# An attention layer whose turned keys lie with their tokens side by side, and whose half-zero query tiles are kept

## The chip, the cores and the metric

The kernel runs on one core of a Trainium2 chip. Its engines are TensorE (PE, with its weight loads as PEld), VectorE (DVE), ScalarE (ACT), GpSimd (POOL), and SyncE (SP), which here only issues transfers; 16 DMA engines move data between DRAM and the core's memory. The metric is the time on the device in microseconds (us), median of several executions.

## The reference

One decoder layer over 1024 tokens of width 1024, in 32-bit floats: a token mixer of attention heads beside a short gated convolution, then a squared-ReLU MLP.

```python
z = rms_norm(x, g_mix_norm) @ w_in          # q, six k/v pieces, gates, conv channels
q = rms_norm(q.reshape(B, T, 8, 64), g_q)   # 8 heads of 64, 2 groups of keys
k_cmp = rms_norm(compress(kc, ...), g_k[0]) # one key per 16 tokens, from blocks of 32
k_slc = rms_norm(ks_, g_k[1])               # selected branch: the 16 best blocks of 64 tokens
k_win = rms_norm(kw_, g_k[2])               # window branch: the last 512 tokens
o = gate0 * softmax(q k_cmp) v_cmp + gate1 * softmax(q k_slc) v_slc + gate2 * softmax(q k_win) v_win
mixed = concat(rms_norm(o, g_out[:512]), rms_norm(conv_out, g_out[512:]))
x = x + mixed @ w_o
x = x + square(relu(rms_norm(x, g_ffn_norm) @ w_up)) @ w_down
```

With 1024 tokens there are only 16 blocks of 64, so the selected branch takes all of them. The softmax scores carry a penalty for distance, and everything is causal.

## The kernel before, in words

**Arithmetic.** A product of 32-bit floats is made of three matmuls: each operand is split into a rounded high part and the rest, and high x high, high x low and low x high are added (`mm3`). Where a tile is called `...h` and `...l`, these are the two parts.

**Stages.** The tokens are taken in 8 blocks of 128. First the input projection (`z_tokens`, and the products `zZ`, `zX`, `zW` for the convolution's channels), with the work on keys and values beside it. Then attention: for each block and group, scores on PE, softmax on DVE, ACT and POOL, turns of the probabilities on PE (`tp`), and their product with the values (`ot`). Then the output projection and the MLP (`X` and `Z` products with `we`, `uu`), which takes about half of the time.

**Keys.** `k_norm` (line 843) normalises the keys of one block of 128 tokens for one branch (`krow`, 128 tokens x 128 numbers: 2 halves of 32 dimensions for 2 groups), and turns them on DVE in squares of 32 x 32 into `kturn`, of which there is one buffer. One store per block and branch puts `kturn` into the DRAM tile `k_d` (line 680), 512 bytes per partition. There are 16 such stores of 64 KB. `v_split` stores the values in the same manner into `v_d`. Before attention, lines 1186 to 1196 load everything back: the keys into four tiles `kn` (two branches x two halves of 512 tokens: `kn00` and `kn01` are the selected branch, `kn10` and `kn11` the window branch), four loads of 128 KB each, 32 partitions with 16 pieces of 256 bytes; the values into `vs` and `vw`, 1 MB each. `split_keys` (line 1204) rounds a `kn` tile into the high part `KH` on ACT and puts the rest into `KL` on DVE, once for each group, so eight times in all.

**Queries.** `queries` (line 1318) loads four pieces `qx` per block and group, copies them into `Qg` (the queries' high part in one half of the partitions, the low part in the other), and makes `Qz`, of which only the group's own half is filled: it clears the other half on POOL, then copies the own one from `Qg`. `Qz` is a ring of two buffers; each of the 16 tiles is cleared anew.

**Scores.** `scores` (line 1234) multiplies `KH` by `Qg` and `KL` by `Qz` into an accumulator `s_`, of which there are two. DVE reads it, adds the penalty and takes the maximum (`pt`, with `nm` the negative maximum), and ACT takes the exponential. PE can't start a third score before DVE has read the first.

**`wc`.** The output projection of the convolution's half (line 1360 on) doesn't need attention. Its 192 matmuls are spread among the first scores. They need `rconv`, made from a few short products `s_<-ones,sqs`. The results are added to tiles `xt` or `y`, which are loaded from x.

**What sets the order.** Every operation is recorded as a node (`Plan`, line 156 on), so almost everything shows as line 273 in the profile and must be told apart by its tiles. A planner (`best`, line 581) then builds an order for all engines by a list schedule, with a cost for each operation and a reckoning of when each transfer lands; `plan.slack` (line 490) adds to that landing, in the reckoning alone. The numbers in `SEEDS` (line 153) each shake the priorities of some operations at random, one after another (`shaken`, line 565). The result is emitted as it stands: every engine takes its instructions in that order. SP issues nearly all loads and stores in one queue in order; a load whose tile isn't free yet holds up all that stand behind it. The `kn`, `qx` and `V` tiles take the space of tiles that the products `zZ` use, so the first of these loads waits until the last `zZ` is done.

Of the kernel before, what the change touches and what calls it, by code (L numbers as in the profile page):

```python
# [10 lines left out]
F32 = mybir.dt.float32  # L11
F32R = mybir.dt.float32r
# [7 lines left out]
P = 128  # L20
T = 1024
# [4 lines left out]
G = 2  # L26
R = H // G
HD = 64
AW = H * HD
CW = D - AW  # L30
NCMP = T // 16
# [118 lines left out]
        self.seen, self.nodes, self.tile = [], [], None  # L150


SEEDS = (1, 23, 31, 38, 41, 62, 71, 73, 75, 77, 80, 88, 104, 105, 109, 117, 124, 125, 127, 128, 139, 177, 192, 197, 199, 200, 266, 277, 284, 301, 314, 374, 375, 379, 394, 395, 403, 428, 451, 473, 489, 497, 527, 539, 602, 635, 663, 668, 683, 688, 735, 738, 757, 795, 807, 960, 974, 981, 1033, 1087, 1174, 1207, 1227, 1240, 1266, 1330, 1456, 1463, 1494, 1514, 1524, 1530, 1663, 1704, 1707, 1772, 1800, 1878, 2113, 2223, 2390, 2423, 2489, 2544, 2549, 2570, 2574, 2706, 2765, 2808, 2860, 2976, 2978, 3198, 3470, 3483, 3569, 3710, 3726, 3799, 3961, 4024, 4169, 4173, 4281, 4302, 4454, 4464, 4536, 4631, 4816, 4942, 5475, 5732, 5800, 5998, 6019, 6274, 6308, 6361, 6542, 6590, 6629, 6638, 6652, 6763, 6768, 6849, 6898, 6926, 6933, 7427, 7431, 7843, 8840, 8935, 9098, 9312, 9425, 9449, 9490, 9543, 9796, 10243, 10373, 10450, 10719, 10753, 10755, 10988, 11031, 11263, 11298, 11337, 11378, 11468, 11734, 11858, 11860, 12512, 12525, 12556, 12899, 12910, 12948, 13367, 13696, 13855, 13915, 13972, 14164, 15272, 15349, 15386, 15617, 16147, 16281, 16952, 16985, 17425, 17652, 17676, 17915, 18093, 18097, 18255, 18325, 18342, 18702, 18971, 19150, 19474, 19616, 21193, 21235, 21388, 21680, 21948, 22334, 23213, 23339, 23611, 23843, 24118, 24207, 24710, 24756, 24876, 25684, 25805, 26155, 26173, 26856, 27014, 28405, 28909, 29650, 29975, 30412, 30442, 30461, 30772, 31961, 32809, 33604, 33968, 34207, 35108, 35382, 35516, 35716, 35789, 36229, 36353, 36557, 36875, 38880, 39359, 39872, 39943, 39989, 40863, 40948, 40951, 41904, 43210, 43597,)


class Plan:
# [437 lines left out]
    def issue(self):  # L594
        end, order = self.schedule(self.best(SEEDS)[1])
        if len(order) < len(self.nodes):
            raise Exception("not all scheduled")
        self.end = end
        with self.tc.manual_schedule(engines=ENGINES):
            for n in order:  # L600
                for f in n.do:
                    f()
        self.done = True
# [3 lines left out]
def trunk_layer(ctx, tc, x, x_t, vectors, w_in, g_qk, w_cmp1, b_cmp1, w_cmp2, b_cmp2,  # L607
                w_o, w_up, w_down, out):
    plan = Plan(tc)
    nc = plan.nc  # L610
# [18 lines left out]
    def copy_act(o, i, scale=1.0):  # L629
        nc.scalar.activation(o, i, AF.Copy, scale=scale)  # L630
# [37 lines left out]
    def rsqrt(o, ss, n, scale):  # L668
        t = st.tile([P, n], F32, name="rs_t", tag=f"rs{n}")
        nc.vector.tensor_scalar(t, ss, scale, EPS, op0=ALU.mult, op1=ALU.add)  # L670
        nc.gpsimd.tensor_tensor(o, t, mhalf[:, :n], op=ALU.pow)

    yacc = {}
    dram = pool(ctx, "dram", space=DRAM)
# [2 lines left out]
    x1_d = dram.tile([T, D], F32, name="x1_d")  # L677
    x2_d = dram.tile([T, D], F32, name="x2_d")
    t_d = dram.tile([T, D], F32, name="t_d")
    k_d = [dram.tile([T, G * HD], F32, name=f"k_d{br}") for br in range(2)]  # L680
    v_d = {br: dram.tile([T, G * 2 * HD], F32, name=f"v_d{br}") for br in "sw"}
    u_d = [dram.tile([7, P, 512], F32, name=f"u_d{q}") for q in range(NPAIR)]

# [158 lines left out]
    with b1:  # L842
        def k_norm(src, br, tb):
            dst = zt.tile([P, 2, G, 32], F32, name="krow")
            sq = zt.tile([P, HD], BF16, name="ksq", bufs=2)
            ss = st.tile([P, G], F32, name="kss")
            for g in range(G):
                c = slice(g * HD, (g + 1) * HD)
                nc.scalar.activation(sq, src[:, c], AF.Square, accum_out=ss[:, g:g + 1])
            ri = st.tile([P, G], F32, name="kri")  # L850
            rsqrt(ri, ss, G, 1.0 / HD)
            for g in range(G):
                nc.vector.scalar_tensor_tensor(dst[:, :, g], src[:, g * HD:(g + 1) * HD].rearrange("p (j d) -> p j d", j=2),
                                               ri[:, g:g + 1], gk_bc[:, br].rearrange("p (j d) -> p j d", j=2),
                                               op0=ALU.mult, op1=ALU.mult)
            turned = zt.tile([P, G * HD], F32, name="kturn", bufs=1)
            nc.vector.transpose(turned, dst.rearrange("p j g d -> p (j g d)"))
            nc.sync.dma_start(k_d[br - 1][tb * P:(tb + 1) * P], turned)

        def v_split(src, br, tb):  # L860
            v = zt.tile([P, G, 2, HD], F32R, name="vrow")
# [112 lines left out]
        for tb, ps in (a for tbs in (QUADS[1], (0,), (1,), (2,), (3,)) for a in z_tokens(pieces, tbs, 512, steps, 1)):  # L974
# [4 lines left out]
            for h in range(H):  # L979
                c = slice(h * HD, (h + 1) * HD)  # L980
# [40 lines left out]
    with ExitStack() as b2:  # L1021
# [10 lines left out]
        def half_tile(name):  # L1032
            return cz.tile([P, 512], F32, name=name, tag="ct", bufs=3)
# [100 lines left out]
        for c in (0, 2):  # L1134
            vs = [u_pair(c + i) for i in range(2)]
            v = [[a[:, th * 512:(th + 1) * 512] for th in range(2)] for a in vs]
            for name, ps in channels(C_CONV + 2 * CW + c * P, C_CONV + 2 * CW + (c + 1) * P):
# [14 lines left out]
                elif name == "S1":  # L1152
                    a = half_tile("ca")
# [28 lines left out]
        def y_tile(shape, name):  # L1182
            return yp.tile(shape, F32, name=name, tag="y", bufs=6)

        V = {br: vp.tile([P, NT, G, 2, HD], F32R, name=f"v{br}", tag=f"v{br}") for br in "sw"}
        kn = {}
        for qd in range(2):
            for br in range(2):
                kn[br, qd] = y_tile([P, 16, G, 32], f"kn{br}{qd}")
                for c in range(4):  # L1190
                    nc.sync.dma_start(kn[br, qd][c * 32:(c + 1) * 32].rearrange("p t g d -> p t (g d)"),
                                      k_d[br][qd * 512:(qd + 1) * 512, c % 2 * HD:c % 2 * HD + HD].rearrange(
                                          "(t p) n -> p t n", p=32))
        for br in "sw":
            nc.sync.dma_start(V[br].rearrange("p t g a d -> p t (g a d)").bitcast(F32),
                              v_d[br].rearrange("(t p) n -> p t n", p=P))
        kp_stack = ExitStack()
        kp = pool(kp_stack, "kp")
        KW = NCMP + 2 * T
# [2 lines left out]
        half = [slice(g * HD, (g + 1) * HD) for g in range(G)]  # L1202

        def split_keys(g, c0, n, ps):
            kh, kl = KH[g][:, c0:c0 + n], KL[:, c0:c0 + n]
            if n == 512:
                kh, kl = [a.rearrange("p (t d) -> p t d", d=32) for a in (kh, kl)]
            copy_act(kh, ps)
            tt(nc.vector, kl[half[g]], ps[half[g]], kh[half[g]].bitcast(F32), ALU.subtract)
        d_sw = kp.tile([P, 1152], F32, name="d_sw")  # L1210
# [8 lines left out]
                                base=0, channel_multiplier=-1)  # L1219

        def k_transposes(g, br, qd):
            split_keys(g, NCMP + br * T + qd * 512, 512, kn[br, qd][:, :, g])

        plan.plus = 20.0
        for g in range(G):
# [4 lines left out]
        psC = pool(cps_stack, "psC", space=PSUM, side="right")  # L1230
        psS_stack = ExitStack()
        psS = pool(psS_stack, "psS", bufs=2, space=PSUM)
        q_load = []
        def scores(tb, g, Qt, filler, po=640):
            Qg, Qz = Qt
            W = (tb + 1) * P
# [81 lines left out]
        def queries(tb):  # L1318
            Qs = []
            for g in range(G):  # L1320
                qx = kp.tile([P, 4, R, 32], F32, name="qx", bufs=1)
                for c in range(4):
                    q_load.append(nc.sync.dma_start(
                        qx[c * 32:(c + 1) * 32].rearrange("p b r t -> p b (r t)"),
                        q_d[tb * P:(tb + 1) * P, (4 * g + c) * P:(4 * g + c + 1) * P].rearrange("(b p) n -> p b n", b=4)))
                Qg = kp.tile([P, R, P], F32R, name="Qg", bufs=3)
                Qz = kp.tile([P, R, P], F32R, name="Qz", bufs=2)
                copy_act(Qg.rearrange("p r (b t) -> p b r t", b=4), qx)
                nc.gpsimd.memset(Qz[half[1 - g]].bitcast(F32), 0.0)
# [18 lines left out]
        for it, tb in [*enumerate(ORDER)][6:] + [*enumerate(ORDER)][:6]:  # L1348
            xt = xq.tile([P, D], F32, name="xt") if it >= 6 else y_tile([P, D], f"y{tb}")
            nc.sync.dma_start(xt, x2d[tb * P:(tb + 1) * P])  # L1350
            t = slice(tb * P, (tb + 1) * P)
            for nh in range(2):
                n = slice(nh * 512, (nh + 1) * 512)
                tag, bufs = (("ot", 2), ("ot", 2), ("ms", 1))[(it * 2 + nh) % 3]
# [28 lines left out]
    with ExitStack() as c_:  # L1383
# [280 lines left out]
        for tb in late[:-1]:  # L1664
            t = ez.tile([P, 512], F32, name="t", tag="t")
# [144 lines left out]
    for c in range(NPAIR // CHUNK):  # L1810
# [6 lines left out]
        for p in range(7):  # L1817
# [17 lines left out]
            ih, n = ACC[p]  # L1835
            for j in range(4):
# [58 lines left out]
```

## Time and profile before

| what | value |
| --- | --- |
| median of 3 runs | 1191.03 us (1188.57 to 1192.53) |
| profiled execution, its own time | 1190.73 us |
| its span, first instruction to last | 1189.0 us |
| granted clock of PE, mean | 0.997 |
| loads of `kn`: 16 of 128 KB, median from issue to landing | 5.3 us |
| stores of `k_d`: 16 of 64 KB, the same | 2.3 us |
| loads of `qx`: 64 of 64 KB, the same | 2.1 us |
| clears of `Qz` on POOL: 16, mean | 521 ns |

The page's groups give an engine, an operation and its tiles (numbers left out), the count, the busy time and the mean of one. Rows of windows give for each engine the busy time and, in brackets, the number of instructions; then the granted clock (PEclk, 1.00 is full), the share of the DMA engines (over 1 where packets overlap) and GB/s. A row of waits names the instruction that waited, what it waited for, and the total, the count and the longest in us. Rows of the timeline and of the chain begin with start and length in us.

### The profile page before, as it was taken

How to read it: one execution, taken by the hardware profiler on the slowest of the kernel's cores; microseconds unless marked ns; L12 is line 12 of the kernel's file. 1: busy time of each engine (PE TensorE's matmuls, PEld its weight loads, DVE VectorE, ACT ScalarE, POOL GpSimd, SP SyncE). 2: the span in 40 equal slices, each digit the busy share in tenths (PEclk: the TensorE clock that was granted, in tenths of full speed). 3: DMA queues.
4: the chain of work that ended last, by engine and by line, in shares of the span. 5: the costliest groups of instructions: out<-in, count | busy, mean ns of one | idle time of the engine just before them, and what ended most of it. 6: DMA issues, size and time to landing. Idle time of an engine off the chain costs nothing.

```text
span 1189.0 us, 18003 instructions
## 1 busy us (share of the span) xinstructions
PE 1176.9 (99%) x5766; PEld 979.4 (82%) x5766; DVE 916.3 (77%) x1827; ACT 700.7 (59%) x1550; POOL 722.9 (61%) x663
## 2 busy tenths in 40 slices
PE   9999999999999999999999999999999999999998
PEld 7888878887878888888788888888888888888887
DVE  8868877785789999998985664554478979887875
ACT  7877635453689988888855554546345444444441
POOL 1544400022266554545878888787799999888971
PEclk9999999999999999999999999999999999999999
DMA  9845521268121101104045445353469545453513
GB/s 342 207 140 169 176 56 48 71 137 249 45 72 46 45 28 63 55 18 141 20 170 193 134 158 186 116 185 113 171 223 388 147 145 175 162 169 100 175 45 141
DMA packets 115102, 161.28 MB, mean 136 GB/s; under 512 B 21472, under 2 KB 68960, under 8 KB 115008
## 3 DMA queue, kind: packets, MB, share of 16 engines
q1 hardware_dynamic: 108752, 152.44, 39.8%
q10 hardware_dynamic: 5520, 5.28, 1.3%
q0 software_dynamic: 736, 2.43, 0.7%
q8 instruction: 45, 0.74, 0.2%
q14 instruction: 49, 0.40, 0.1%
HBM read 111.87 MB, written 48.23 MB: 135 GB/s over the span
## 4 chain that ended last, share of the span: by engine, by line
PE 89%; DVE 4%; ACT 4%; DMA 2%; issue 1%; SPq 0%; POOL 0%; POOLq 0%; ACTq 0%
PE X L273 28%; PE Z L273 18%; PE zp L273 9%; PE zX L273 5%; PE ot L273 5%; PE tp L273 4%; PE wa L273 3%; PE W L273 3%; PE zZ L273 3%; PE wc L273 2%; PE zW L273 1%; DMA w_raw<-in_w_in_dram 1%; PE hp L273 1%; ACT wu L273 1%; DVE pl L273 1%; DMA vs<-v_ds 1%
## 5 line engine op out<-in xcount | busy, mean ns | idle before, releaser
L273 PE MATMUL X<-we,uu 128*128 128x512 f32 (+1 forms) x726 | 200.9, 388 | 0.0
L273 PE MATMUL Z<-we,uu 128*128 128x512 f32 (+1 forms) x576 | 166.2, 388 | 0.0
L273 PEld LDWEIGHTS X<-we,uu 128*128 128x128 f32 x726 | 136.0, 188 | 28.2 <-DVE y L273 0.2
L273 ACT ACTIVATE uu<-ur 128x512 fp32r<-128x512 f32 x108 | 67.2, 629 | 122.0 <-PE Z L273 72.0
L273 PEld LDWEIGHTS Z<-we,uu 128*128 128x128 f32 x576 | 107.9, 188 | 22.3
L273 DVE TENSOR_TENSOR y<-X,y 128x512 f32<-128x512 f32 x129 | 87.1, 683 | 33.2 <-PE X L273 32.3
L273 ACT ACTIVATE pt<-pt,nm 128x640 f32<-128x640 f32 (+7 forms) x128 | 93.7, 734 | 29.9 <-DVE nm L273 29.7
L273 POOL TENSOR_TENSOR d<-d 128x512 f32<-128x512 f32 x64 | 98.8, 1562 | 8.4 <-DVE d L273 7.8
L273 DVE TENSOR_TENSOR pl<-tp,ph 128x512 fp32r<-128x512 f32 (+1 forms) x148 | 94.8, 656 | 7.5 <-ACT ph L273 7.0
L273 PE MATMUL tp<-ident,pt 128*128 128x128 f32 x528 | 93.0, 274 | 0.0
L273 ACT ACTIVATE ph<-tp 128x512 fp32r<-128x512 f32 (+1 forms) x148 | 80.9, 573 | 15.5 <-PE tp L273 11.5
L273 POOL TENSOR_TENSOR uu<-ur,uu 128x512 fp32r<-128x512 f32 x54 | 80.8, 1501 | 4.9 <-ACT uu L273 4.9
L273 ACT ACTIVATE we<-s 128x512 fp32r<-128x512 f32 x55 | 34.8, 632 | 81.5 <-PE X L273 40.4
L273 DVE TENSOR_TENSOR y<-Z,y 128x512 f32<-128x512 f32 x96 | 64.9, 681 | 21.2 <-PE Z L273 20.7
L273 PEld LDWEIGHTS tp<-ident,pt 128*128 128x128 f32 x528 | 67.5, 141 | 11.2 <-PE tp L273 0.3
L273 POOL MEMSET Qz<- 64x512 f32 x16 | 8.3, 521 | 107.0 <-PE zZ L273 102.9
L273 PE MATMUL zp<-w_lo,hTh 128*128 128x512 f32 (+1 forms) x192 | 67.0, 362 | 0.0
L273 PE MATMUL zp<-w_hi,hTh 128*128 128x512 f32 (+1 forms) x192 | 66.6, 363 | 0.1
L273 PE MATMUL zp<-w_hi,hTl 128*128 128x512 f32 (+1 forms) x192 | 66.0, 360 | 0.0
L273 DVE TENSOR_TENSOR we<-wu,we 128x512 fp32r<-128x512 f32 x38 | 48.5, 1290 | 20.5 <-PE X L273 10.8
L273 POOL TENSOR_TENSOR we<-wd,we 128x512 fp32r<-128x512 f32 x32 | 48.1, 1502 | 24.7 <-ACT we L273 24.3
L273 POOL TENSOR_TENSOR pt<-pt,rr 128x640 f32<-128x640 f32 (+4 forms) x64 | 62.9, 1009 | 0.0
(1353 smaller groups left out, 3611.5 us busy)
## 6 DMA issues: line engine op xcount, KB each, us to landing
u_d<-d SPq DMA_DIRECT2D x112, 256.0 KB, 3.3
ur<-u_d SPq DMA_DIRECT2D x108, 256.0 KB, 2.7
wu<-in_w_up_dram SPq DMA_DIRECT2D x16, 1024.0 KB, 5.8
wd<-in_w_down_dram SPq DMA_DIRECT2D x16, 1024.0 KB, 7.2
xt<-in_x_dram SPq DMA_DIRECT2D x10, 512.0 KB, 5.9
x<-in_x_t_dram SPq DMA_DIRECT2D x16, 256.0 KB, 6.2
w1r<-in_w_cmp_dram SPq DMA_DIRECT2D x16, 256.0 KB, 3.0
q_d<-qn SPq DMA_DIRECT2D x8, 512.0 KB, 3.0
```

Source lines behind the costliest of these rows:

```text
L273: node.do.append(lambda: getattr(engine, method)(*[real(x) for x in a], **{k: real(x) for k, x in kw.items()}))
```

## The change

The DRAM tiles `k_d` now hold 32 dimensions x 2 halves x 2 groups x 1024 tokens, so that the tokens of one dimension lie side by side. `k_norm` stores each `kturn` in four parts, one for each 32 partitions, in pieces of 32 tokens (128 bytes); there are 64 stores of 16 KB. Each of the 16 loads of `kn` reads 32 partitions with two pieces of 512 tokens (2 KB). The `kn` tiles have the tokens in a straight row, so `split_keys` needs no strips of 32. The planner's reckoning of the landings gets 2.0 us of slack for the `kn` loads and 3.0 for the `V` loads, where there was none. The ring `Qz` becomes two kept tiles, `Qz0` for the first group and `Qz1` for the second; each one's other half is cleared when the tile is made, and later blocks only write the half that they use. And `SEEDS` is another list.

```diff
@@ -150,7 +150,7 @@
         self.seen, self.nodes, self.tile = [], [], None
 
 
-SEEDS = (1, 23, 31, 38, 41,
...
+SEEDS = (9, 10, 14, 31, 37,
...
 
 
 class Plan:
@@ -677,7 +677,7 @@
     x1_d = dram.tile([T, D], F32, name="x1_d")
     x2_d = dram.tile([T, D], F32, name="x2_d")
     t_d = dram.tile([T, D], F32, name="t_d")
-    k_d = [dram.tile([T, G * HD], F32, name=f"k_d{br}") for br in range(2)]
+    k_d = [dram.tile([32, 2, G, T], F32, name=f"k_d{br}") for br in range(2)]
     v_d = {br: dram.tile([T, G * 2 * HD], F32, name=f"v_d{br}") for br in "sw"}
     u_d = [dram.tile([7, P, 512], F32, name=f"u_d{q}") for q in range(NPAIR)]
 
@@ -855,7 +855,10 @@
                                                op0=ALU.mult, op1=ALU.mult)
             turned = zt.tile([P, G * HD], F32, name="kturn", bufs=1)
             nc.vector.transpose(turned, dst.rearrange("p j g d -> p (j g d)"))
-            nc.sync.dma_start(k_d[br - 1][tb * P:(tb + 1) * P], turned)
+            for b in range(4):
+                t = tb * P + b * 32
+                nc.sync.dma_start(k_d[br - 1][:, :, :, t:t + 32].rearrange("p j g t -> p (j g) t"),
+                                  turned[b * 32:(b + 1) * 32].rearrange("p (n t) -> p n t", t=32))
 
         def v_split(src, br, tb):
             v = zt.tile([P, G, 2, HD], F32R, name="vrow")
@@ -1186,14 +1189,16 @@
         kn = {}
         for qd in range(2):
             for br in range(2):
-                kn[br, qd] = y_tile([P, 16, G, 32], f"kn{br}{qd}")
+                kn[br, qd] = y_tile([P, G, 512], f"kn{br}{qd}")
+                plan.slack = 2.0
                 for c in range(4):
-                    nc.sync.dma_start(kn[br, qd][c * 32:(c + 1) * 32].rearrange("p t g d -> p t (g d)"),
-                                      k_d[br][qd * 512:(qd + 1) * 512, c % 2 * HD:c % 2 * HD + HD].rearrange(
-                                          "(t p) n -> p t n", p=32))
+                    nc.sync.dma_start(kn[br, qd][c * 32:(c + 1) * 32], k_d[br][:, c % 2, :, qd * 512:(qd + 1) * 512])
+                plan.slack = 0.0
+        plan.slack = 3.0
         for br in "sw":
             nc.sync.dma_start(V[br].rearrange("p t g a d -> p t (g a d)").bitcast(F32),
                               v_d[br].rearrange("(t p) n -> p t n", p=P))
+        plan.slack = 0.0
         kp_stack = ExitStack()
         kp = pool(kp_stack, "kp")
         KW = NCMP + 2 * T
@@ -1203,8 +1208,6 @@
 
         def split_keys(g, c0, n, ps):
             kh, kl = KH[g][:, c0:c0 + n], KL[:, c0:c0 + n]
-            if n == 512:
-                kh, kl = [a.rearrange("p (t d) -> p t d", d=32) for a in (kh, kl)]
             copy_act(kh, ps)
             tt(nc.vector, kl[half[g]], ps[half[g]], kh[half[g]].bitcast(F32), ALU.subtract)
         d_sw = kp.tile([P, 1152], F32, name="d_sw")
@@ -1219,7 +1222,7 @@
                                 base=0, channel_multiplier=-1)
 
         def k_transposes(g, br, qd):
-            split_keys(g, NCMP + br * T + qd * 512, 512, kn[br, qd][:, :, g])
+            split_keys(g, NCMP + br * T + qd * 512, 512, kn[br, qd][:, g])
 
         plan.plus = 20.0
         for g in range(G):
@@ -1230,7 +1233,7 @@
         psC = pool(cps_stack, "psC", space=PSUM, side="right")
         psS_stack = ExitStack()
         psS = pool(psS_stack, "psS", bufs=2, space=PSUM)
-        q_load = []
+        q_load, zeroed = [], []
         def scores(tb, g, Qt, filler, po=640):
             Qg, Qz = Qt
             W = (tb + 1) * P
@@ -1324,9 +1327,11 @@
                         qx[c * 32:(c + 1) * 32].rearrange("p b r t -> p b (r t)"),
                         q_d[tb * P:(tb + 1) * P, (4 * g + c) * P:(4 * g + c + 1) * P].rearrange("(b p) n -> p b n", b=4)))
                 Qg = kp.tile([P, R, P], F32R, name="Qg", bufs=3)
-                Qz = kp.tile([P, R, P], F32R, name="Qz", bufs=2)
+                if g == len(zeroed):
+                    zeroed.append(kp.tile([P, R, P], F32R, name=f"Qz{g}"))
+                    nc.gpsimd.memset(zeroed[g][half[1 - g]].bitcast(F32), 0.0)
+                Qz = zeroed[g]
                 copy_act(Qg.rearrange("p r (b t) -> p b r t", b=4), qx)
-                nc.gpsimd.memset(Qz[half[1 - g]].bitcast(F32), 0.0)
                 nc.gpsimd.tensor_copy(Qz[half[g]], Qg[half[g]])
                 Qs.append((Qg, Qz))
             return Qs
```

The names in the rows below carry the planner's own numbers; a wait in brackets names the semaphores of the engine or DMA queue.

On PE, where the channel products `zZ` and `zX` end and the `wc` products begin (the loads of `qx` and `kn` wait for the last `zZ`), there stood before:

```order
L273 MATMUL zZ_2643<-hTl1_125,wcuh_2834 128x512
L273 MATMUL zZ_2643<-hTh1_126,wcul_2840 128x512
L273 MATMUL zX_2622<-t4h_186,wcuh_2861 128x512 [waits DVE_49,Activation_49]
L273 MATMUL zX_2622<-t4l_185,wcuh_2861 128x512
L273 MATMUL zX_2622<-t4h_186,wcul_2863 128x512
```

and there stands after the change:

```order
L273 MATMUL zX_2665<-t4h_186,wcuh_2900 128x512
L273 MATMUL zX_2665<-t4l_185,wcuh_2900 128x512
L273 MATMUL zX_2665<-t4h_186,wcul_2902 128x512
L273 MATMUL zZ_2689<-hTl1_125,wcuh_2894 128x512
L273 MATMUL zZ_2689<-hTh1_126,wcul_2896 128x512
L273 MATMUL wc_2801<-hTh0_190,MCh_2186 128x512
```

The last `zZ` stood ahead of 12 `zX` products, and now stands behind them; between it and the first score there were 12 `zX`, 41 `wc` and 8 short products, and there are 32 `wc` and 8 short ones.

On SP, at the end of the key loads, there stood before:

```order
L273 DMA kn11_2921<-k_d1_210 32x16x64 [waits DMAHW7_49]
L273 DMA vs_2942<-v_ds_209 128x8x256 [waits DMAHW0_49]
L273 DMA y1_3079<-in_x_dram 128x1024 [waits DMAHW1_49,DVE_49]
L273 DMA qx_3082<-q_d_215 32x4x128 [waits DMAHW2_49,Activation_49]
L273 DMA qx_3082<-q_d_215 32x4x128 [waits DMAHW3_49]
L273 DMA kn11_2921<-k_d1_210 32x16x64 [waits DMAHW4_49]
L273 DMA kn01_2920<-k_d0_211 32x16x64 [waits DMAHW5_49]
L273 DMA qx_3082<-q_d_215 32x4x128 [waits DMAHW6_49]
L273 DMA kn11_2921<-k_d1_210 32x16x64 [waits DMAHW7_49]
L273 DMA kn11_2921<-k_d1_210 32x16x64 [waits DMAHW0_49]
L273 DMA y0_3102<-in_x_dram 128x1024 [waits DMAHW1_49,DVE_49]
L273 DMA vw_2941<-v_dw_208 128x8x256 [waits DMAHW2_49]
```

and there stands after the change:

```order
L273 DMA kn11_2975<-k_d1_210 32x2x512 [waits DMAHW5_49,DVE_49]
L273 DMA kn11_2975<-k_d1_210 32x2x512 [waits DMAHW6_49]
L273 DMA vs_2996<-v_ds_209 128x8x256 [waits DMAHW7_49]
L273 DMA vw_2995<-v_dw_208 128x8x256 [waits DMAHW0_49]
L273 DMA kn11_2975<-k_d1_210 32x2x512 [waits DMAHW1_49]
L273 DMA qx_3183<-q_d_215 32x4x128 [waits DMAHW2_49,Activation_49]
L273 DMA y0_3188<-in_x_dram 128x1024 [waits DMAHW3_49,DVE_49]
L273 DMA qx_3183<-q_d_215 32x4x128 [waits DMAHW4_49]
L273 DMA qx_3183<-q_d_215 32x4x128 [waits DMAHW5_49]
L273 DMA kn11_2975<-k_d1_210 32x2x512 [waits DMAHW6_49]
```

The last piece of `kn11` stood ahead of `vw`, and now stands behind both `vs` and `vw`.

On DVE, where the last keys are split (`KL`) between the reads of the scores (`pt`), there stood before:

```order
L273 ISA pt_3038,nm_80<-s__3156,d_sw_2937 128x256
L273 ISA nm_80 128x1
L273 TENSOR_TENSOR KL_2938<-kn01_2920,KH1_2939 64x512 [waits DMAHW5_49,Activation_49]
L273 TENSOR_TENSOR KL_2938<-kn01_2920,KH0_2940 64x512 [waits DMAHW6_49,DMAHW4_49]
L273 TENSOR_TENSOR KL_2938<-kn11_2921,KH1_2939 64x512 [waits DMAHW7_49,DMAHW0_49,Activation_49]
L273 TENSOR_TENSOR KL_2938<-kn11_2921,KH0_2940 64x512 [waits DMAHW7_49,DMAHW4_49,Activation_49]
L273 ISA pt_3038,nm_80<-s__3176,d_sw_2937,nm_80 128x256 [waits DVE_49,PE_49]
```

and there stands after the change:

```order
L273 ISA pt_3090,nm_80<-s__3293,d_sw_2991 128x512 [waits PE_49]
L273 ISA nm_80 128x1
L273 TENSOR_TENSOR KL_2992<-kn11_2975,KH1_2993 64x512 [waits DMAHW6_49,DMAHW1_49,Activation_49]
L273 SCALAR_TENSOR_TENSOR xt_3180<-wc_3008,rconv_64,xt_3180 128x512 [waits DMAHW0_49,DMASW4_49]
L273 ISA pt_3090,nm_80<-s__3264,d_sw_2991,nm_80 128x256
L273 ISA nm_80 128x1
L273 SCALAR_TENSOR_TENSOR xt_3180<-wc_3010,rconv_64,xt_3180 128x512
L273 TENSOR_TENSOR KL_2992<-kn11_2975,KH0_2994 64x512 [waits DMAHW5_49,Activation_49]
L273 SCALAR_TENSOR_TENSOR y0_3188<-wc_3308,rconv_64,y0_3188 128x512 [waits PE_49]
```

Four subtractions stood one behind the other; each now stands among reads of scores and of `wc`.

More of the change, by code (lines that the diff above doesn't have):

```diff
@@ L150, in __init__ @@
         self.seen, self.nodes, self.tile = [], [], None
-SEEDS = (1, 23, 31, 38, 41, 62, 71, 73, 75, 77, 80, 88, 104, 105, 109, 117, 124, 125, 127, 128, 139, 177, 192, 197, 199, 200, 266, 277, 284, 301, 314, 374, 375, 379, 394, 395, 403, 428, 451, 473, 489, 497, 527, 539, 602, 635, 663, 668, 683, 688, 735, 738, 757, 795, 807, 960, 974, 981, 1033, 1087, 1174, 1207, 1227, 1240, 1266, 1330, 1456, 1463, 1494, 1514, 1524, 1530, 1663, 1704, 1707, 1772, 1800, 1878, 2113, 2223, 2390, 2423, 2489, 2544, 2549, 2570, 2574, 2706, 2765, 2808, 2860, 2976, 2978, 3198, 3470, 3483, 3569, 3710, 3726, 3799, 3961, 4024, 4169, 4173, 4281, 4302, 4454, 4464, 4536, 4631, 4816, 4942, 5475, 5732, 5800, 5998, 6019, 6274, 6308, 6361, 6542, 6590, 6629, 6638, 6652, 6763, 6768, 6849, 6898, 6926, 6933, 7427, 7431, 7843, 8840, 8935, 9098, 9312, 9425, 9449, 9490, 9543, 9796, 10243, 10373, 10450, 10719, 10753, 10755, 10988, 11031, 11263, 11298, 11337, 11378, 11468, 11734, 11858, 11860, 12512, 12525, 12556, 12899, 12910, 12948, 13367, 13696, 13855, 13915, 13972, 14164, 15272, 15349, 15386, 15617, 16147, 16281, 16952, 16985, 17425, 17652, 17676, 17915, 18093, 18097, 18255, 18325, 18342, 18702, 18971, 19150, 19474, 19616, 21193, 21235, 21388, 21680, 21948, 22334, 23213, 23339, 23611, 23843, 24118, 24207, 24710, 24756, 24876, 25684, 25805, 26155, 26173, 26856, 27014, 28405, 28909, 29650, 29975, 30412, 30442, 30461, 30772, 31961, 32809, 33604, 33968, 34207, 35108, 35382, 35516, 35716, 35789, 36229, 36353, 36557, 36875, 38880, 39359, 39872, 39943, 39989, 40863, 40948, 40951, 41904, 43210, 43597,)
@@ new lines @@
+SEEDS = (9, 10, 14, 31, 37, 43, 46, 49, 54, 68, 70, 74, 107, 115, 118, 124, 143, 145, 157, 206, 249, 280, 368, 373, 374, 417, 464, 546, 570, 623, 736, 745, 786, 810, 813, 823, 861, 862, 906, 909, 954, 974, 988, 1030, 1076, 1154, 1174, 1225, 1255, 1273, 1300, 1317, 1347, 1402, 1461, 1485, 1601, 1619, 1665, 1686, 1848, 2094, 2096, 2150, 2251, 2333, 2370, 2409, 2509, 2549, 2652, 2657, 2723, 2774, 2798, 2806, 2808, 2997, 3518, 3652, 3659, 3711, 3735, 3925, 3954, 4024, 4077, 4131, 4200, 4291, 4519, 4760, 4847, 4856, 4935, 5005, 5018, 5047, 5103, 5280, 5566, 5615, 5641, 5682, 5687, 5765, 5891, 5986, 5992, 6060, 6216, 6693, 6760, 6809, 7027, 7033, 7071, 7146, 7175, 7218, 7280, 7329, 7334, 7402, 7535, 7905, 7969, 8109, 8202, 8392, 8652, 8712, 8840, 9459, 9821, 10135, 10276, 10404, 10564, 10648, 10794, 10827, 10846, 10961, 11029, 11779, 11921, 12016, 12073, 12076, 12103, 12156, 12417, 12447, 12696, 13311, 13367, 14174, 14375, 15022, 16052, 16279, 16461, 16738, 16988, 17063, 17218, 17559, 17781, 17796, 17853, 17944, 18000, 18082, 18133, 18151, 18986, 19395, 19399, 20229, 20262, 20400, 20403, 20427, 20499, 20525, 20568, 20636, 21205, 22128, 23333, 23357, 23426, 24133, 24223, 24459, 24585, 24701, 24734, 24742, 25129, 25482, 25598, 26188, 26260, 26760, 26765, 26773, 26820, 27078, 27155, 27656, 27714, 29392, 29548, 29664, 29841, 30200, 30702, 30743, 31148, 32071, 33501, 34699, 35971, 37026, 37231, 38010, 38669, 38771, 38800, 39151, 41399, 42375, 42964, 42993, 43101, 43619, 44193, 44269, 44427, 45317, 47117, 47322, 47824, 49333, 52152, 52427, 52631, 52684, 52725, 52914, 52942, 53498, 53847, 53886, 53961, 54004, 54035, 54235, 54717, 54737, 55944, 56210, 56567, 56696, 57118, 59403, 61639, 61909, 62133, 62571, 63768,)
```

## Prediction

> **What bounds the kernel now.** I read the page's first part, then the waits of the matrix engine (PE), then windows of the trace around the two largest.
>
> ```profile
> span 1189.0 us, 18003 instructions
> PE 1176.9 (99%) x5766; PEld 979.4 (82%) x5766; DVE 916.3 (77%) x1827; ACT 700.7 (59%) x1550; POOL 722.9 (61%) x663
> ...
> engine line waited for: us in total, times, longest us
> PE s__3210 L273 <- DVE nm L273: 2.2, 1, 2.2
> PE warm L273 <- POOL ident L273: 1.4, 1, 1.4
> PE s__3861 L273 <- DVE nm L273: 1.4, 1, 1.4
> ```
> PE is busy for 99% of the span, so nothing that is made shorter on another engine counts unless PE stops for it. There are two places inside the kernel where PE stops for over 1 us (`warm` is the start): it waits for VectorE (DVE) to empty a score accumulator `s_`.
>
> ```profile
> core 0: us, PE busy (x) PEld busy (x) DVE busy (x) ACT busy (x) POOL busy (x), PEclk, DMA share, GB/s
> 259.30:262.40 3.10, 3.01 (x21) 2.84 (x22) 2.00 (x7) 0.00 (x0) 0.34 (x1) 1.00 1.20 228
> 278.90:281.20 2.30, 0.14 (x2) 0.03 (x1) 1.85 (x5) 0.94 (x3) 0.00 (x0) 1.00 1.10 352
> 281.60:285.00 3.40, 3.40 (x11) 2.70 (x10) 2.02 (x9) 2.13 (x6) 1.21 (x2) 0.50 1.05 382
> 339.60:343.00 3.40, 3.40 (x13) 2.82 (x12) 2.92 (x10) 2.53 (x8) 2.95 (x5) 0.50 0.27 77
> 350.00:550.00 200.00, 199.83 (x1227) 171.80 (x1226) 185.19 (x649) 172.39 (x402) 105.81 (x170) 1.00 0.15 51
> ```
> Behind each of the two waits stands a stretch of 3.4 us with a granted clock of 0.50 (281.6 to 285.0 and 339.6 to 343.0): a wait costs its own length and then 3.4 x (1 - 0.5) = 1.7 us. From 350 to 550 us PE is busy for 199.83 of 200 us: nothing is to be had there. The change bears on the first wait, whose cause is in the chain of work that ended last, followed back from it (start, us, what):
>
> ```profile
> 264.06 8.00 DMA vs<-v_ds
> 272.07 0.02 issue
> 272.08 6.55 DMA kn<-k_d
> 278.63 0.02 issue
> 278.65 0.64 ACT KH L273
> 279.29 0.02 issue
> 279.31 0.70 DVE KL L273
> 280.01 0.02 issue
> 280.04 0.68 DVE KL L273
> 280.72 0.40 DVE pt L273
> ```
> The last piece of the turned keys `kn` lands at 278.63; ScalarE (ACT) rounds it, DVE subtracts twice, and then only reads the accumulator (`pt`) that PE has wanted since 279. The DMA engines are full there (share 1.05 to 1.20, a sum over overlapping packets). How much they move differs: 228 GB/s at a share of 1.20 from 259.3 to 262.4, mostly key pieces of 256 B, and 382 at 1.05 from 281.6, longer pieces; per unit of share 190 and 364.
>
> **The change, part by part.**
> *Key loads.* The 16 loads carry 16 x 131,072 B = 2.10 MB. At 190 GB/s that is 11.0 us of full DMA engines, at 364 it is 5.8: 5.3 us less before the last piece, if pieces of 2 KB move as the long ones do. The wait is 2.16 us long, so the DMA time covers it. The new order, though, puts more ahead of the last piece: both V tiles (1 MB each) and five tiles of x, about 7.5 MB from the first load instead of 5.7. At 364 to 382 GB/s, counted with the 9 to 10 us of keys and queries at the head, I estimate its landing 25 to 27.5 us after the first issue. It was 278.63 - 251.25 = 27.4.
>
> ```profile
> 250.83 0.39 PE L273 MATMUL zZ<-hTh,wcul 128*128 128x512 f32 x1
> 251.06 0.39 PE L273 MATMUL zX<-t4h,wcuh 128*128 128x512 f32 x1
> ...
> 259.39 1.50 PE L273 MATMUL s__2960<-ones,sqs 128*128 128x1 f32 x12
> ...
> 265.83 0.31 PE L273 MATMUL s__2961<-KH,Qg 128*128 128x320 f32 x1
> ...
> 251.25 0.33 SPq L273 DMA_DIRECT2D qx<-q_d  x1
> ...
> 255.55 2.46 SPq L273 DMA_DIRECT2D kn<-k_d  x4
> ...
> 264.22 0.63 ACT L273 ACTIVATE Qg<-qx 128x512 fp32r<-128x512 f32 x1 [0.55 <-DMA qx<-q_d]
> 265.03 1.15 ACT L273 ACTIVATE KH<-kn 128x512 fp32r<-128x512 f32 x2 [0.17 <-DMA kn<-k_d]
> ```
> What decides is when PE and DVE want it. One matmul follows another after 251.06 - 250.83 = 0.23 us. In the new order 40 instead of 61 matmuls stand between the last `zZ`, whose end releases the loads, and the first score: 32 `wc` and 8 short ones. With the 1.85 us that the short ones took, and the 0.42 us from zZ's start to the first issue, the cover is 33 x 0.2275 + 1.85 - 0.42 = 8.9 us; it was 265.83 - 251.25 = 14.6. The last piece's subtractions stand among the later score reads, 72 `wc` (16.4 us) and 20 scores further on. The scores have 256 to 512 columns, in proportion 0.11 to 0.23 us each, 2.3 to 4.6 us: 27.6 to 29.9 us after the first issue. With 1.3 us of ACT and DVE work behind a landing at 25 to 27.5 that is a microsecond short at the worst, three and a half to spare at the best. And the four subtractions, adjacent before, are now spread among the `pt` reads, so one late piece no longer holds a read by two of them (0.70 + 0.68 us). I take the 2.16 us wait as gone, with its 1.70 of half clock.
>
> ```profile
> L273 SPq DMA_DIRECT2D kn<-k_d x16: 423/486/1327, 251.6 to 272.1; - x16
> ...
> DMA to landing us min/median/max: 2.6/5.3/7.1
> ```
> *The shorter cover.* What is late next is the first score. It needs four `qx` and four `kn00` pieces, all now within the first nine issues. The ninth issue of the old order, within the four from 255.55, came at about 256.2, 4.9 us after the first, and the quickest key piece landed 2.6 us after its issue: 7.5 us, then 0.63 for `Qg` and 0.64 for `KH`, 8.8 us against 8.9. It is barely covered; a miss of 1 us would cost 1 us, and from about 1.4 us on (the shorter of the two waits above) the half clock as well. I take 0 and keep 0 to 2.6 + 1.7 = 4.3, the upper end being a landing at the median of 5.3 instead of 2.6.
>
> ```profile
> L273 SPq DMA_DIRECT2D k_d<-kturn x16: 319/322/587, 31.1 to 150.3; - x16
> ...
>   DVE kturn L273: 5.5, 3
> ...
> 50.00:70.00 20.00, 20.00 (x92) 16.32 (x91) 8.65 (x24) 11.89 (x50) 6.42 (x10) 1.00 0.67 165
> 119.00:155.00 36.00, 35.59 (x212) 30.84 (x211) 32.27 (x92) 20.68 (x70) 12.56 (x18) 1.00 0.55 161
> ...
> kv_d<-z ACTq DMA_DIRECT2D x8, 128.0 KB, 3.8
> v_ds<-vrow SPq DMA_DIRECT2D x8, 128.0 KB, 3.7
> ```
> *Key stores.* 16 stores become 64; 48 more issues of 0.32 us are 15.4 us of the sync engine's queue (SP), about 1 us per token block, ahead of the weight loads that stand behind them. The turned block `kturn` has one buffer, so the next transpose on DVE waits until all four land; such waits were 5.5 us in three. The first branch's stand where DVE is busy 8.65 of 20 us, and there PE lost nothing. The second branch's stand where DVE is busy 32.27 of 36: seven following transposes, each at worst 1.0 us later (three further issues), minus the 36 - 32.27 = 3.7 us that DVE has free, is 3.3. In the new order 5 to 17 DVE instructions stand between two of them, so most land in time: I take 0.2, bounds 0 to 3.3. No row shows pieces of 128 B; the nearest are `kv_d`, pieces of 256 B, and `v_ds`, 1 KB, 128 KB each: 3.8 and 3.7 us, no difference. The Trainium skill, "DMA: Bandwidth & Descriptors", Specifications, speaks against these stores: under 512 B a transfer is read, modified and written back. By it they would land later and the sum would move toward its 3.3; the pair at 3.8 and 3.7 does not bear it out for 256 B, and no row shows it at 128.
>
> ```profile
> L273 POOL MEMSET Qz<- 64x512 f32 x16 | 8.3, 521 | 107.0 <-PE zZ L273 102.9
> ```
> *Query tiles.* 14 of the 16 clears go, 14 x 0.521 = 7.3 us of GpSimd (POOL). They lie in the stretch where POOL is busy 105.8 of 200 us and PE 199.83 of 200: 0. Were that cover gone, at most the first clear would show, which is kept.
> *Rounding of the keys* reads a straight row instead of 16 strips of 32. The old form took 0.64 and 0.68 to 0.70 us; between half of that (eight of each: 5 us off ACT, off the path) and no change I take no change: 0.
> *Order.* The list of seeds is another one, so all engines' orders are rebuilt. The slack terms change only the planner's reckoning. The second wait (1.37 + 1.7 = 3.1 us, at 337.6) comes where DVE is busy 2.92 of 3.4 us; it depends on the order alone and could stay, go, or grow. I take it as unchanged, bounds -3.1 to +2.
>
> *Sum*, against the profiled execution (1190.73 us with a span of 1189.0; the runs' median is 1191.03, 0.3 us more): 1190.73 - 2.16 - 1.70 + 0.2 = **1187.1**. The Trainium skill, "TensorE: Matmul & The Clock Gate", "Why this matters for your kernels", asks only that PE has no idle gaps over about 3 us. By it a gap of 2.16 would leave the clock alone and the sum would be 1190.73 - 2.16 + 0.2 = 1188.8. The trace differs: clock 0.50 right behind gaps of 2.16 and 1.37 us.
>
> **The rivals.**
> *The second wait goes too*: 1187.1 - 3.1 = 1184.0. For it: fewer DVE conflicts in attention's start, an order chosen anew. Against it: DVE is nearly full there, and nothing in the change takes work from it.
> *The wait moves*: the first score is late, or a transpose or weight load behind the 64 stores, by 1.0 to 2.6 us with its half clock: 1187.1 + 2.7 to 4.3 = 1189.8 to 1191.4. For it: cover 8.9 against 8.8 needed. Against it: the first score's eight loads are now the first of their queue but for one, where `kn00`'s last was the fourteenth before.
> *Keys do not land faster* (slower than before). If 2 KB pieces move no faster than the old ones, the change does not do what it says. `kn00` reached ACT at 265.03, 13.8 us after the first issue; with 0.64 of `KH` that is 14.4 against a cover of 8.9, so PE waits 5.5 us at the first score, plus 1.7 of half clock; the 1.8 MB more ahead of the last piece (4.8 us at 382 GB/s) make that some 1.4 us late as well: 1187.1 + 7.2 + 0 to 1.4 = 1194.3 to 1195.7, say 1195.0. It decides from a wait of 5.5 us on. Against it: 364 GB/s per unit of share of the long pieces, and nine issues instead of fourteen for the first score, whatever a piece costs.
>
> **How the numbers follow.** This kernel's measurement can tell about 0.3%, 3.6 us, from no change. Forecast 0.54 (its own range 1186.0 to 1190.3, with the stores' upper bound; 0.31 of it beyond 0.3%, 0.23 within, since 1187.1 lies 3.6 below); second wait gone 0.17, faster; wait moved 0.19, within; keys not faster 0.10, slower. So faster 0.48, same 0.42, slower 0.10. The range goes from 1183.0 (the second rival case and a microsecond of small waits) to 1193.0 (the moved wait with half of the stores' bound); the last rival lies outside.
>
> **What would show it.** Right: no PE wait for `nm` near 280 us and no clock of 0.50 behind it; key loads landing in 2 to 3 us; `Qz` cleared twice; `kturn` waits of DVE without a PE wait beside them. Wrong: a PE wait at the first score (`KH` or `Qg`), at the last `kn` piece behind the V tiles, or for weights between 119 and 155 us; or a gap of 2 us without the half clock.

## The result, and the profile after

The changed kernel takes 1200.01 us (median of 4 runs, 1197.25 to 1201.46), the kernel before 1190.46 beside it. The ratio is 1.0085, with a 95% interval of 1.007 to 1.0099: about 10 us slower, where 1187.1 was forecast with a range that ended at 1193.0. First the page of the changed kernel, then what PE waited for.

```profile
span 1197.0 us, 18038 instructions
...
PE 1178.2 (98%) x5766; PEld 975.4 (81%) x5766; DVE 915.7 (76%) x1827; ACT 698.6 (58%) x1550; POOL 722.9 (60%) x649
...
engine line waited for: us in total, times, longest us
PE zW L273 <- DVE wcul L273: 2.6, 1, 2.6
PE tp L273 <- DMA ch<-kv_d: 2.0, 1, 2.0
PE wc L273 <- DVE y L273: 1.5, 1, 1.5
PE warm L273 <- POOL ident L273: 1.4, 1, 1.4
PE wc L273 <- DVE xt L273: 1.3, 1, 1.3
PE zp L273 <- ACT hTh L273: 1.0, 1, 1.0
```

Both waits for `nm` that were over 1 us are gone, as hoped for the first, and a new set has come: for the split weights `wcul` and the loaded `ch`, long before attention, and for the tiles `y` and `xt` within it. Windows of both kernels tell how much each stage lost; first the kernel before, then the changed one (busy time of the engines, the granted clock, the share of the DMA engines, GB/s).

```profile
0.00:25.00 25.00, 23.48 (x101) 18.83 (x102) 19.89 (x37) 17.81 (x27) 2.69 (x17) 1.00 0.96 347
50.00:75.00 25.00, 25.00 (x119) 20.62 (x118) 12.33 (x30) 16.74 (x73) 9.04 (x12) 1.00 0.66 163
125.00:150.00 25.00, 24.97 (x144) 21.60 (x143) 21.97 (x62) 14.91 (x50) 10.03 (x14) 1.00 0.56 166
250.00:350.00 100.00, 95.46 (x476) 78.37 (x475) 75.84 (x209) 58.57 (x134) 37.38 (x60) 0.97 0.50 137
```

```profile
0.00:25.00 25.00, 22.37 (x94) 17.47 (x95) 18.82 (x34) 16.68 (x25) 2.95 (x17) 1.00 0.95 341
50.00:75.00 25.00, 22.78 (x103) 18.09 (x102) 10.64 (x25) 12.76 (x47) 10.23 (x15) 1.00 0.64 152
125.00:150.00 25.00, 22.56 (x158) 20.75 (x156) 20.51 (x60) 13.39 (x51) 9.10 (x12) 1.00 0.58 151
250.00:350.00 100.00, 95.64 (x474) 76.97 (x473) 75.36 (x199) 55.80 (x124) 30.20 (x44) 1.00 0.48 140
258.00:358.00 100.00, 94.86 (x479) 76.08 (x478) 73.19 (x202) 56.42 (x131) 36.49 (x53) 1.00 0.48 140
```

PE's idle time grew by 1.1 us at the start, by 2.2 from 50 to 75 us and by 2.4 from 125 to 150. The 1.1 us at the start vary between executions of one order: x1, which has the changed kernel's order, is idle for 1.55 us there, the kernel before for 1.52. From 250 to 350 is where the faster key loads were to pay. By then the changed kernel is 7 to 8 us behind, so the last row, 8 us later, is the one to compare: PE is idle for 5.1 us there, 0.6 more than before. Only the clock was won, which is full there and had not been. The stages that lost most are those of the key stores. Their tile:

```profile
L273 SPq DMA_DIRECT2D k_d<-kturn x64: 555/597/1827, 33.8 to 163.5; - x64
...
  DMA k_d<-kturn: 10.4, 7
...
DMA to landing us min/median/max: 1.8/2.7/6.8
```

Each of the 64 issues takes 0.60 us, not 0.32 as the 16 did, although it carries a quarter of the bytes. DVE waits 10.4 us, in seven places, for stores to land before it may turn the next block; 6.3 us of it are one wait between 50 and 80 us. The chain of work behind the wait for `wcul`, followed back from 150 us (start, us, what), shows what that does:

```profile
137.36 3.04 DMA k_d<-kturn
...
140.49 0.31 DVE kturn L273
...
143.94 1.92 DMA k_d<-kturn
...
145.94 0.31 DVE kturn L273
...
149.50 0.61 DVE wcul L273
```

DVE cannot turn a block until the last store of the former one has landed; the split of the weights stands behind that on the same engine, and PE waits for it. And in attention, the chain back from the wait for `xt`:

```profile
279.21 13.63 DMA vw<-v_dw
...
292.91 6.67 DMA xt<-in_x_dram
...
299.67 0.22 DVE xt L273
```

The two 1 MB loads of the values stand ahead of the last x tiles and keys in SyncE's queue; `vw` lands at 292.85, and only then is the load of `xt` issued. The reason is in SP's order rows: the loads wait on eight semaphores in turn, DMAHW0 to DMAHW7, so that each is issued only when the transfer eight places before it has landed. `xt` stands eight places behind `vw`, and a tile `y` eight behind `vs`: it was issued at 289.08, when `vs` had landed (278.67 + 10.4).

### The profile page after: what moved, and what is told of

Read it like the earlier page. It is cut to its first block, busy times and chain, and to the rows that moved or that the text cites. A ratio compares the mean times of both kernels' runs of the same rounds, so it can differ in the third digit from the quotient of the medians.

```text
span 1197.0 us, 18038 instructions
## 1 busy us (share of the span) xinstructions
PE 1178.2 (98%) x5766; PEld 975.4 (81%) x5766; DVE 915.7 (76%) x1827; ACT 698.6 (58%) x1550; POOL 722.9 (60%) x649
## 4 chain that ended last, share of the span: by engine, by line
PE 81%; DMA 3%; ACT 1%; DVE 1%; SPq 1%; POOL 1%; issue 1%; DVEq 0%; ACTq 0%; POOLq 0%
PE X L273 29%; PE Z L273 18%; PE tp L273 6%; PE ot L273 5%; PE zX L273 5%; PE wa L273 4%; PE W L273 4%; PE zZ L273 3%; PE wc L273 1%; PE zW L273 1%; DMA vw<-v_dw 1%; DMA kn<-k_d 1%; SPq L273 1%; DMA xt<-in_x_dram 1%; DMA k_d<-kturn 0%
```

## The experiments

In all of them the planner gets the recorded operations of the one kernel or the other, so that PE, DVE, ACT and POOL run the same instructions in the same order as there ("old order", "new order"); only what is named is exchanged when the operations are emitted. A ratio is to the kernel before on the same chip, with its 95% interval; differences in us between runs are of their medians. The kernel before took 1189.71 to 1190.64 us on the chips used, so a difference between chips is good to about 1 us.

| run | order | keys | stores a block | second place | values | median us | ratio |
| --- | --- | --- | --- | --- | --- | --- | --- |
| before | old | old | 1 | no | early | 1190.46 | 1 |
| changed | new | new | 4 | no | early | 1200.01 | 1.0085 (1.0070 to 1.0099) |
| x1 | new | new | 1 | no | early | 1195.0 | 1.0052 (1.0039 to 1.0065) |
| x2 | new | old | 1 | no | early | 1196.5 | 1.0064 (1.0050 to 1.0077) |
| x3 | old | new | 4 | no | early | 1200.64 | 1.0098 (1.0084 to 1.0111) |
| x4 | old | new | 1 | no | early | 1196.27 | 1.0051 (1.0037 to 1.0064) |
| x5 | new | new | 4 | yes | early | 1192.93 | 1.0024 (1.0012 to 1.0036) |
| x6 | old | new | 4 | yes | early | 1193.9 | 1.0031 (1.0021 to 1.0042) |
| x7 | old | new | 1 | yes | early | 1188.42 | 0.9980 (0.9969 to 0.9992) |
| x8: kept query tiles | old | old | 1 | no | early | 1190.74 | 0.9996 (0.9986 to 1.0006) |
| x9 | old | old | 1 | yes | early | 1189.62 | 0.9993 (0.9981 to 1.0005) |
| x10 | new | new | 4 | yes | behind | 1190.13 | 0.9998 (0.9988 to 1.0009) |
| x11 | old | new | 1 | yes | behind keys | 1190.01 | 0.9998 (0.9987 to 1.0009) |
| x12 | new | new | 1 | yes | early | 1192.24 | 1.0009 (1.0000 to 1.0018) |
| x13 | new | new | 4 | no | behind | 1195.83 | 1.0044 (1.0028 to 1.0060) |
| x14 | new | old | 1 | yes | behind | 1191.15 | 1.0005 (0.9995 to 1.0015) |
| x15 | new | new | 1 | yes | behind | 1189.18 | 0.9990 (0.9982 to 0.9999) |
| x16 | old | new | 1 | yes | behind x | 1191.76 | 1.0007 (0.9995 to 1.0019) |

### Stores, pieces or order: x1 to x4

The first theories were that the number of stores loads SyncE's queue (S), that pieces of 128 B are slow (P), or that the new order is the worse one (O). x1 sends the four stores as one; x2 has the old layout's stores, loads and strips in the new order; x3 and x4 bring the new layout's loads and tiles into the old order, x3 with its four stores, x4 with one. The diff is x1's.

```diff
-            for b in range(4):
-                t = tb * P + b * 32
-                nc.sync.dma_start(k_d[br - 1][:, :, :, t:t + 32].rearrange("p j g t -> p (j g) t"),
-                                  turned[b * 32:(b + 1) * 32].rearrange("p (n t) -> p n t", t=32))
+            nc.sync.dma_start(
+                k_d[br - 1][:, :, :, tb * P:(tb + 1) * P].rearrange("p j g (b t) -> b p (j g) t", b=4),
+                turned.rearrange("q (n t) -> q n t", t=32))
```

> The changed kernel with every engine's order kept as it is, but the four stores of a turned key block sent as one store of 64 KB (the same 128 B pieces), issued where the last of the four stood: 16 store issues instead of 64. Theory S (the 48 further stores hold up SyncE's queue, by their issue time of about 0.6 us each and by the transfers allowed in flight, and the loads behind them come late): the waits of PE for ch, w1h, wcul before 165 us go, about 8 us less than the changed kernel, 1190 to 1192. Theory P (pieces of 128 B are slow, whatever the count of stores): no gain, 1198 to 1200. Theory O (the new list of seeds made a worse order): no gain, 1198 to 1200.

> The changed kernel with every engine's order kept, but the keys in the old layout: 16 stores with 512 B pieces where the last of the four stood, loads in 256 B pieces, split in strips of 32. Only the order, the slack and the kept query tiles are left of the change. Theory S: the early waits go, 1190 to 1193 (with late keys perhaps 2 more). Theory P: the same. Theory O: still 1198 or more.

> The kernel before with every engine's order kept, but the keys stored by four stores each (128 B pieces, issued one behind the other where the one store stood), loaded in 2 KB pieces and split as a straight row. Theory S: the stores cost 5 to 9 us before 165 us and the faster loads give back the 2.16 us wait and its half clock: 1192 to 1197. Theory P: the same range. Theory O: faster than before, about 1187.

> The kernel before with every engine's order kept, the new layout of the keys with loads in 2 KB pieces, but each turned block sent as one store of 64 KB in 128 B pieces. Theory S: the stores cost nothing, the loads give 3.9 us: 1186 to 1188. Theory P: the small pieces cost the same as in the changed kernel, 1192 to 1197. Theory O: 1186 to 1188 as in S.

None of the three came through whole. x1 gained 5 us by the medians and 4 by the ratios, of the 8 that S wanted, and met no range. x2, without a single new store, was still 0.6% slower than before, which spoke for O, though it stayed short of O's 1198; but x3, in the old order, was as slow as the changed kernel and slower than any theory said, which spoke against O. x4 met P's range and refuted S. What x3 and x4 share stands in their tile of the turned block; the first line is x3's time of DVE waiting before a transpose and the count, the second x4's.

```profile
  DMA k_d<-kturn: 16.2, 8
```

```profile
  DMA k_d<-kturn: 11.1, 6
```

It was 5.5 in three before. So a fourth theory, M1: `kturn` has one buffer, DVE must wait until its stores have landed, and four issues in a row, or one that takes longer, lengthen that by more than DVE has to spare. Its rival M2 is what is left of S: the 64 issues themselves hold up the loads.

### A second place for the turned block: x5 to x9

Every second block is turned into a tile that is idle then: `kcn` for the first branch, half of `g_bc` for the second. x8 tries the kept query tiles alone.

```diff
             turned = zt.tile([P, G * HD], F32, name="kturn", bufs=1)
+            own = turned.base.node.do[0]
+
+            def place(b=turned.base):
+                flip[br] = flip.get(br, 0) + 1
+                if flip[br] % 2:
+                    own()
+                else:
+                    b.tile = kcn.base.tile if br == 1 else g_bc.base.tile[:, 0:2].rearrange("p a d -> p (a d)")
+            turned.base.node.do = [place]
```

> The changed kernel with every engine's order kept, but every second turned key block goes to other memory (of tiles that are idle then), so that DVE's transpose waits for the stores of the block before the last, not of the last. Theory M1 (the one buffer makes DVE wait until all four stores have landed, and the weight splits wcul, wcuh behind it come late): DVE's kturn waits (10.4 us in seven) go, and with them PE's waits for wcul and wcuh between 140 and 165 us (2.6, 0.5 and 0.4 us): 1195.5 to 1197. Theory M2 (the SyncE queue with 64 store issues makes the loads late): no change, 1199 to 1201.

> x3 (old order, new layout, four stores a block) with the same second place for turned blocks. M1: PE's waits for wcul and wcuh (1.9, 1.7 and 1.7 us, and the half clock behind one) go: 1193 to 1196; the wait for ch (2.9 us) stays. M2: 1199 to 1201.

> x4 (old order, new layout, one store of 128 B pieces a block) with the same second place for turned blocks. M1: the waits for wcuh and wcul (1.8 and 1.2 us) go, and the loads' gain of 4 us stands: 1188 to 1193, level with or faster than before. M2: 1195 to 1197.

> The kernel before with every engine's order kept, but the two half-zero query tiles kept and cleared twice instead of sixteen times; 14 clears are left out. If the clears lie beside other work, as argued: no change, 1188 to 1192. If GpSimd's time mattered in attention: up to 7.3 us faster, 1183.

> The kernel before (old layout, old order) with only the second place for turned blocks. If its own kturn waits of DVE (5.5 us in three) are beside PE's work, as argued: no change, 1189 to 1191. If the second place by itself is what made x7 faster: 1187 to 1188.5.

Theory M1 holds three times over: x5 is 7.1 us faster than the changed kernel (more than forecast), x6 6.7 faster than x3, x7 7.9 faster than x4, each with nothing but the second place added. x9 shows that the place alone gives the kernel before nothing that can be told: its 5.5 us of waits were covered. With it, 128 B pieces in one store cost nothing that shows beside the loads (x7, 0.9980, against x9, 0.9993), so P falls too as an account of the loss. M2 keeps a part in the old order: x6, with 64 issues, still waits 2.6 us for `ch` and is 5.5 us slower than x7, which has 16 and does not wait. x8 is level: the clears were beside other work.

What is left in x5 is the wait list's first rows:

```profile
PE tp L273 <- ACT pt L273: 2.8, 1, 2.8
PE wc L273 <- DVE y L273: 1.5, 1, 1.5
...
PE wc L273 <- DVE xt L273: 1.3, 1, 1.3
```

The waits for `wcul` and `ch` are gone; those for `y` and `xt`, behind the values, stand.

### The values' place in the queue: x10 to x13

Theory V is that the values' loads make the last keys and x tiles late, E that the rest is the engines' order. The two loads are issued later on SyncE, in x10 and x13 behind the last keys and the two x tiles after them. In the changed kernel `vs` is first used at 321.1 us.

```diff
             for n in order:
-                for f in n.do:
-                    f()
+                if n not in self.values:
+                    for f in n.do:
+                        f()
+                if n is behind:
+                    for v in self.values:
+                        for f in v.do:
+                            f()
```

> x5 (the changed kernel with a second place for turned blocks), and the two 1 MB loads of the values moved in SyncE's queue from the middle of the last keys to behind the two x tiles after them; every other engine's order kept. Theory V (the values ahead of the last keys and x tiles make these late, and DVE and PE wait): PE's waits for y and xt (1.5 and 1.3 us) go, 1188.5 to 1190.5. Theory E (the loss that is left lies in the engines' order): no change, 1192 to 1194.

> The changed kernel with only the values' two loads moved behind the last keys and the two x tiles after them (no second place for turned blocks). If the two causes add up: about 2.8 us less than the changed kernel, 1196.5 to 1198. If the values only matter when the turned buffer is cured: no change, 1199 to 1201.

> x7 (old order, new layout, one store a block, second place for turned blocks), and the values' loads moved in SyncE's queue behind the last key piece and the x tile after it. Theory V: the last piece lands about 2.9 us earlier (1 MB at 364 GB/s), the wait of 2.2 us for the score accumulator goes: 1185 to 1187. Theory E: no change, 1188 to 1189.

> x1 (the changed kernel, one store a block) with the second place for turned blocks: x5 with 16 store issues instead of 64. If the count of stores costs time of its own beside the buffer, as in the old order (x6 against x7, 5.5 us): 1188 to 1190.5. If in the new order the buffer was all of it: 1192 to 1194.

x10 is 2.8 us faster than x5 and level with the kernel before; in its list only the first of x5's three waits is left, shorter (what made that one was not followed):

```profile
PE tp L273 <- ACT pt L273: 1.8, 1, 1.8
PE warm L273 <- POOL ident L273: 1.4, 1, 1.4
PE tp L273 <- POOL pt L273: 0.8, 1, 0.8
```

x13, with the values' move alone, gains 4.2 us, more than expected, so the two are nearly separate causes: 7.1 and 4.2 alone, 9.9 together. x12 answers for the count of stores in the new order: with the second place, 16 issues in place of 64 bring 0.7 us by the medians (1192.24 against 1192.93) and 1.8 by the ratios, with intervals that overlap. x11 was a miss. The wait that it was meant to remove is in x7's list as the first line here, and gone in x11's, whose first is the second line:

```profile
PE s__3202 L273 <- DVE nm L273: 2.2, 1, 2.2
```

```profile
PE wc L273 <- DVE xt L273: 1.9, 1, 1.9
```

A wait of 1.9 us for an x tile, which now stood behind the values, took its place.

### Is the faster load worth anything: x14 to x16

x14 has x10's order and both cures, but the keys in the old layout; x15 has one store a block; x16 puts the values in the old order behind that x tile too.

```diff
-            behind = loads[last + 1]
+            behind = loads[last + 4]
```

> x10 with the keys in the old layout (16 stores with 512 B pieces, loads in 256 B pieces, strips of 32), order, second place and the values' move kept. If the layout's faster loads are worth what was forecast (3.9 us, less what 64 stores cost): 1192 to 1195, slower than x10. If the faster loads are hidden in this order: 1189 to 1191, level with x10 or faster.

> x10 with one store a block instead of four. If the count of stores is beside PE's work once the buffer is cured: 1189.5 to 1191, as x10. If it still costs: 1187 to 1188.5.

> x11 with the values' loads also behind the x tile for which PE waited 1.9 us there. If the load queue's order hid the keys' gain: that wait goes and no other takes its place, 1185.5 to 1187.5, faster than both kernels. If another wait takes its place: 1188 to 1190.

x14, just above the range for hidden loads, and x10 can't be told apart (1.0005 and 0.9998, intervals that overlap): in this order the faster loads are hidden. x15 is 1 us faster than x10, between the two expectations, with intervals that overlap. x16 is a second miss: the wait for `xt` went, 0.9 us for `y` came, and the time didn't fall. The fastest of all is x7, by 0.1 to 0.3% faster than the kernel before; x9 beside it leaves 0.13%, some 1.5 us, to the layout, with intervals that overlap. x7 also shows where the faster loads were lost. The time of SyncE waiting for `vs` is in x7 the first line, in x9 the second:

```profile
SPq L273 <- DMA vs<-v_ds: 4.7, 1, 4.7
```

```profile
SPq L273 <- DMA vs<-v_ds: 1.1, 1, 1.1
```

In x7 the last key piece stands eight places behind `vs`, and its issue waits for `vs` to land. So the last keys are rounded 28.0 us after the first load is issued, in x9 28.8; in x11, with the values moved, 24.8, and x7's wait for the score accumulator is gone. x3, x4 and x6 wait 2.4 to 2.5 us for `vs` and don't have it either; what else differs there was not tested.

## Why the prediction was wrong

- **The stores**, taken at 0.2 us with bounds 0 to 3.3, were the step that failed first; the term was mis-sized. It went by "48 more issues of 0.32 us" (they took 0.60) and by "each at worst 1.0 us later". The last of four is issued some 1.9 us after the first and lands at least 1.8 later, 3.7 in place of 1.5 to 2.3. "So most land in time" was read from the number of DVE instructions between two transposes, not from their time, and DVE waited 10.4 us. The bound also counted only the second branch: in the stage of the first, where "PE lost nothing" before, PE lost 2.0 us to `ch`. Removing the wait gave 7.1 us (x5). (The 15.4 us of issues are about 1 us per stored block, so 2 per token block, not 1.)
- **The last keys** were the second step. They landed 297.15 - 264.56 = 32.6 us after the first issue, where 25 to 27.5 was estimated. The order rows showed both values' loads ahead of them, and the estimate charged them at full rate, but not that the eighth load behind each waits for it to land: `y` and `xt` came late, and PE waited 1.5 and 1.3 us. Moving the values gave 2.8 us on x5 and 4.2 alone (x10, x13).
- **The faster loads.** "5.3 us less before the last piece" didn't come. The pieces do cost the DMA engines less: in the first 10 us of the loads x7 moved 228 GB/s at a share of 0.80, x9 181 at 0.91. But from the first load's issue to the rounding of the last keys it took 28.0 us in x7 and 28.8 in x9, 31.2 in x10 and 32.9 in x14: 0.8 and 1.7 us less. That landing followed the queue's order and waits, not only what the engines can move.
- **The first score** was in time, as forecast: the first keys were taken up 6.9 us after the first issue, the score began 9.3 us after it, and PE didn't wait.
- **The wait of 2.16 us** and its half clock went, as forecast, and the second wait too. But at this stage PE was idle for 0.6 us more than before, and only the clock was gained, since the waits for `y` and `xt` took its place; with these cured, the layout made no difference that can be told (x14 against x10). The 3.9 us were worked out from one wait, though the one behind it in the same full queue was the next to bind.
- **The query tiles**: 0, as forecast (x8: 0.9986 to 1.0006).
- **The half clock** was priced as certain behind any wait from about 1.4 us on, at 1.7 us. That was wrong: see below.
- **The order**: taken at 0 outside the second wait. By itself it costs 0.64% (x2, 6.8 us on its chip), most of it in attention, where PE is idle for 8.2 us from 250 to 350 against 4.5 before. Nearly all of that is gone with the same two cures (x14, 0.05%), so it is the way in which the new order meets the one buffer and the values' loads; which of the two it is was not run apart in the old layout.
- **The rivals.** "The wait moves" named the mechanism, a transpose or a weight load behind the 64 stores, and gave it one place and 2.6 us; it came in several. "Keys do not land faster" didn't happen as priced: the first keys were not late.

## What to carry to other kernels

A store that is split is not only more issues: where its source has one buffer, the engine that fills it waits for the last of the pieces, and everything queued behind on that engine waits too. So count from the first issue to the last landing, and set it against the time, not the number of instructions, to the next fill. And where a queue lets only so many transfers be under way (here eight), look for the large one in it that is needed last (here 2 MB of values, landed some 30 us early) before making the others faster.

## What the hardware showed that was not expected

The clock after a wait is not told by the wait's length. Behind PE's wait of 2.60 us the changed kernel ran on at full clock; behind 2.97 us at the same place, in x13, it ran at half.

```profile
150.20:153.60 3.40, 3.40 (x15) 2.79 (x16) 3.03 (x11) 1.83 (x7) 1.85 (x3) 1.00 0.18 48
```

```profile
148.60:152.00 3.40, 3.40 (x8) 2.72 (x9) 3.03 (x11) 1.68 (x7) 1.83 (x3) 0.50 0.18 48
```

The wait of 1.37 us at 337 us had 3.4 us of half clock behind it in the kernel before, and none in x16; x7's wait of 2.22 us had none either. The half clock isn't always 3.4 us long: in x13 it held from 148.5 to past 154 us, which costs nearly 3 us. And in x9 it came without a wait: the clock was at 0.50 from 262 to 264.5 us, behind 16 short products, where PE had waited no more than 0.3 us. So a wait between 1.4 and 3 us costs itself, and something more in some runs only. The Trainium skill, "TensorE: Matmul & The Clock Gate", "Why this matters for your kernels", lets gaps up to about 3 us pass; here some of 1.37 and 2.16 us did not.

And the issue time of a store follows its pattern more than its size: 64 KB in rows of 512 B took SyncE 0.32 us, 16 KB in rows of four pieces of 128 B 0.60, and 64 KB in such rows 0.54 (x1).
